# A two-layer encoder trunk: where a head's last norm, the splits, the rotation's sums and the latents' squares are computed

## The chip, the cores and the metric

One core of a Trainium2 chip. The metric is the device time of one execution of the program in microseconds; less is better. A core has engines that run beside each other: TensorE (PE, matmuls and transposes; its weight loads are listed as PEld), VectorE (DVE), ScalarE (ACT), GpSimd (POOL) and SyncE (SP), which here only issues DMA transfers. PE writes to PSUM, which the kernel divides into banks of 128 x 512 fp32 values; the other tiles lie in SBUF.

## The reference, cut to what matters

The model has 1024 tokens of width 1024, in fp32, and two layers. Each is a norm, a shift and scale from a conditioning vector, a token mixer with a SiLU gate, an output projection and a gated residual addition; a last norm closes it.

```python
for i in range(2):
    shift, scale, gate = _modulation(c, ada_w[i], ada_b[i])
    h = _rmsnorm(x, norm_g[i]) * (1.0 + scale) + shift
    y = _diff_attention(h, ...) if i == 0 else _mla(h, ...)
    x = x + gate * y
return _rmsnorm(x, final_norm_g)
```

Layer 0 is differential attention with 8 heads: q and k are rotated by position (`_rope`), each head has two softmaxes of which one is subtracted with a factor, and each head's output gets a norm of its own over its 128 channels:

```python
q, k, v, z = jnp.split(h @ w_in, 4, axis=-1)      # widths 1024 each
p = softmax(q1 k1) - lam * softmax(q2 k2)         # per head
o = _rmsnorm(p @ v, subln_g) * (1.0 - lambda_init)
y = (o.reshape(b, s, 1024) * jax.nn.silu(z)) @ w_out
```

Layer 1 is latent attention: q and k/v come from latents of 384 and 256 channels, and each latent is normed over its channels before it is multiplied on.

## The kernel before, in words

**Precision.** Every fp32 matmul is done as three fp32r matmuls of split operands: high times high, high times low and low times high (`mm3`, lines 182 to 184). So each operand needs a split: ScalarE copies it to a rounded high part, and GpSimd or VectorE subtracts this to get the low part. In `split_raw` (L227, L228) this is done for the projections' weights, in `Seven.put` (L1166, L1167) for the operands of the output projection.

**Order.** The program is written in Python; a planner then fixes each engine's order at build time, from its own simulated times and the order in which things were written. An engine's queue runs strictly in that order. Three helpers bind the planner: `tc.issue_after(ins)` puts what a block writes behind `ins` on the same engine; `behind(eng)` does so with the last copy or subtraction of the attention (`mk["S"]`, `mk["V"]`); `tc.keep_in_program_order(ins)`, in `in_turn`, pins an instruction behind everything written before it on its engine. `mk` is emptied after layer 0's attention, and with that `behind` and `in_turn` bind nothing.

**Layer 0's attention** (`attn0`, from L1002). Per head there are eight query tiles of 128 rows. A tile has two rounds of scores (L844), each with a maximum on VectorE (L397) and an exponential on ScalarE (L399), and VectorE joins the two (L852). One tile later the joined tile is transposed by PE in two groups of four (`transpose_p`, L380), copied by ScalarE (L382) and its low part made by VectorE (L383); two tiles later it is multiplied with v. Between these pieces, `fills` says how many steps of the next head's projections are put in; after each step `side.tick()` runs one entry of a list of side work. `rope` (L312) does the rotation there: ScalarE copies the projection (L319, L321), four DMAs swap its halves (L323), GpSimd multiplies it by the cosine (L324) and the swapped one by the sine (L329), and `fin` adds the two on VectorE (L333). `stack_k` and `stack_q` then split the sum (ScalarE L341, L342, L349, L350; GpSimd L343, L344, L351, L352).

**A head's own norm** (`subln`, L911). PE sums the squares by matmuls with a column of ones (L922), VectorE and GpSimd turn them into factors (L925 to L930, the power at L169), and `finish` (L876) brings the factors to all partitions: by two DMAs through DRAM (L405, L407), GpSimd multiplying after them (L882) and a store (L886), or, for the last half of the last head, which is wanted at once, by four diagonal matrices (VectorE, L899), matmuls with ones into a bank `rb` (L900), and a multiplication on VectorE (L901).

**Output projection of layer 0.** The product is done by Strassen's scheme with seven half-size products (`Seven`). Product n needs left factors A(n, h) and weights W(n, h), h = 0 to 3; for n = 2 to 5 the left factors are sums and differences of heads. `fetch_a` and `fetch_w` load them (L1150, on SP), `split_a` and `split_w` split them. During the last head, `extra0(i)` (L1259) is called after each tile i (8 to 10 are the tail after the eighth): it loads, splits (`both`), and starts `PRE0[i]` portions of products 0 and 1 by `Pre7.step`, one portion being three matmuls of 512 columns into one of two banks. These portions fill PE where the last head has no projections left.

After the attention, the rest of product 0 goes to the y banks 2 and 3, product 1 to two acc banks and two "tr" banks (`Z`, read to x by `add0`, L1376). Meanwhile `tail_b` runs `finish` for the last half head and the four sums and differences made of it (L1332 to L1335), which give A(2, 3) to A(5, 3). Product 2 follows in the y banks 0 to 3, then 3 to 6. In PSUM at this stage: four y banks, two tr banks, two acc banks. `group0` (L1382) norms x for layer 1 (`norm_x`: VectorE L454 or ScalarE L452, on tiles of 128 x 1024), and PE transposes it (L465).

**Layer 1's latents** (`lora`, L1601). Each projection half-strip of eight `mm3` is copied to `craw` and squared (L1611, L1614) by ScalarE; VectorE sums the squares over the latent's strips (L1615). At step `NORM_AT` of the following half, `norm` sums them over the partitions by PE (L1620), and the factors go through DRAM.

Of the kernel before, what the change touches and what calls it, by code (L numbers as in the profile page):

```python
# [16 lines left out]
ALU = mybir.AluOpType  # L17
# [4 lines left out]
P = 128  # L22
# [22 lines left out]
V_LATE = 6  # L45
MODS = (2, 1, 1, 1, 0, 0, 0, 0)
V1_AT = (3, 2)
NORM_AT = 4
PRE0 = (0, 0, 0, 0, 1, 1, 2, 2, 2, 3, 3)
PRE1 = (0, 0, 0, 0, 0, 0, 0, 1, 1, 1, 1)  # L50
LAST1 = (((0, 1), 0, HF), ((2,), 0, HF), ((3,), 0, 256), ((3,), 256, HF))
Z_LAST = 2
# [29 lines left out]
def trunk(ctx: ExitStack, tc: tile.TileContext, A, out):  # L82
# [226 lines left out]
                self.count += 1  # L309
                side.tick()  # L310

    def rope(rp, acc, half, scale, eng=G):  # L312

        cs = slice(half * HF, half * HF + HF)
        raw = rp.tile([P, HF], F32, name="rp_raw", tag="rp", bufs=6)
        sw = rp.tile([P, HF], F32, name="rp_sw", tag="rp", bufs=6)
        r = rp.tile([P, HF], F32, name="rp_r", tag="rp", bufs=6)
        if scale == 1.0:
            S.copy(raw, acc)  # L319
        else:  # L320
            S.mul(raw, acc, scale)  # L321
        for q in range(4):
            SP.dma_start(sw[q * 32 : q * 32 + 32], raw[(q ^ 1) * 32 : (q ^ 1) * 32 + 32])  # L323
        r_ = eng.tensor_mul(r, raw, cosT[:, cs])  # L324
        if eng is G:
            in_turn(r_)

        def rot():
            in_turn(G.tensor_mul(sw, sw, sinT[:, cs]))  # L329

        def fin():
            with behind("V"):
                V.tensor_add(r, r, sw)  # L333
            return r

        return rot, fin
# [38 lines left out]
    def transpose_p(p, pth, ptl, t, kh):  # L375

        tr = bank("tr", "tr", [P, 4, P])
        for j in range(4):
            kt = kh * 4 + j
            PE.transpose(tr[:, j, :], p[:, kt * P : (kt + 1) * P], ident)  # L380
        dst = slice(t * P, (t + 1) * P)
        mk["S"] = S.copy(pth[kh][:, :, dst], tr).ins  # L382
        mk["V"] = V.tensor_sub(ptl[kh][:, :, dst], tr, f32v(pth[kh][:, :, dst])).ins  # L383
# [364 lines left out]

    def k_done(h):
        def f(acc, half):  # L750
            rot, fin = rope(wp, acc, half, 1.0, G if h else V)

            def g():
                t = a0a.tile([P, 2, HF], F32R, name="ks", tag="ks", bufs=4)
                stack_k(t, fin())
                KS.setdefault(h, [None, None])[half] = t

            side.add(*[None] * ROT, rot, *[None] * (DEF - 1 - ROT), g)
        return f

    def q_done(h):
        def f(acc, half):
            rot, fin = rope(wp, acc, half, SC0, G if h else V)

            def g():
                qa = a0a.tile([P, 2, HF], F32R, name="qa", tag="qs", bufs=4)
                qb = a0a.tile([P, 2, HF], F32R, name="qb", tag="qs", bufs=4)
                stack_q(qa, qb, fin())
                QS.setdefault(h, [None, None])[half] = qa, qb

            side.add(*[None] * ROT, rot, *[None] * (DEF - 1 - ROT), g)
        return f
# [103 lines left out]
    def finish(o, y, l, h, half, dst, ap_, dgs):  # L876

        if dst is None:
            b, rb = bcast_rows(ap_, y, "osq", 4)

            def scale():
                in_turn(G.tensor_mul(t3(o), t3(o), rb))  # L882
                hooks.append(lambda: hooks.append(store))

            def store():
                SP.dma_start(oF[l][h, half], o)  # L886

            if l == 0 and (h, half) >= (NH - 2, 1):
                hooks.append(lambda: hooks.append(scale))
            else:  # L890
                hooks.append(scale)
            return
        rb = bank("z" if l else "tr", "rb", [P, HF])
        for j in range(4):
            js = slice(j * P, (j + 1) * P)
            if l:
                S.mul(dgs[:, js], ident, y[:, j : j + 1])
            else:
                V.tensor_scalar(dgs[:, js], ident, y[:, j : j + 1], None, op0=ALU.mult)  # L899
            PE.matmul(rb[:, js], ones, dgs[:, js], start=True, stop=True)  # L900
        V.tensor_mul(o, o, rb)  # L901

    ssq_at = []

    def head_out(o_, o, sq):

# [4 lines left out]
    def subln(o, sq, zz, half, h, dst):  # L911
# [5 lines left out]
            V.tensor_mul(o, o, GZ[h][half])  # L917

        def rest():
            pt = bank("tr", "ssq", [P, HF]) if dst is not None else ssq_at[0] if ssq_at else bank("acc", "ssq")  # L920
            for j in range(4):
                PE.matmul(pt[:, j : j + 1], sq[:, j * P : (j + 1) * P], ones[:, 0:1], start=True, stop=True)  # L922
            w = sm.tile([P, 4], F32, name="sl_w")
            fin = sm.tile([P, 4], F32, name="sl_f")
            V.tensor_mul(fin, zz, zz)  # L925
            V.scalar_tensor_tensor(out=w, in0=fin, scalar=P * EPS / GUARD ** 2, in1=pt[:, 0:4], op0=ALU.mult, op1=ALU.add)  # L926
# [3 lines left out]
            in_turn(G.tensor_mul(y, y, fin))  # L930
# [203 lines left out]
    class Seven:  # L1134
# [12 lines left out]
            self.raws[n, h, "W"] = self.load(self.home_w(n, h), tS[self.l][n, h])  # L1147

        def load(self, home, src):
            self.last = SP.dma_start(f32v(home[1]), src).ins  # L1150
            return *home, f32v(home[1])

        def split_a(self, n, h, eng=V):
# [47 lines left out]
    class Pre7:  # L1201
# [5 lines left out]
        def step(self):  # L1207
# [4 lines left out]
            if not h and not i:  # L1212
# [1 line left out]
                    self.done(self.accs)  # L1214
                self.accs = [bank("acc", "oy") for _ in range(2)]
                ssq_at.append(self.accs[1])
            self.sv.mm(n, self.accs[i], h, i, start=True)
            self.n += 1

    stX, stO = ExitStack(), ExitStack()  # L1220
# [38 lines left out]
    def extra0(i):  # L1259
# [34 lines left out]
        if i == 3:  # L1294
            fw(0, 2)
            fa(0, 2)
            fw(0, 3)
            SP.dma_start(k0["11"], oF[0][3, 0])
        if 3 <= i <= 6:
            both(0, i - 3)  # L1300
        if 4 <= i <= 6:
            fw(1, i - 4)
            fa(1, i - 4)
        if i == 6:
            SP.dma_start(k0["21"], oF[0][3, 1])
            k0["pair"] = [pw.tile([P, HF], F32, name="ob", tag="ob", bufs=4) for _ in range(4)]
        if i == 7:
            fw(1, 3)
            for t, (hh, half) in zip(k0["pair"], ((2, 0), (6, 0), (2, 1), (6, 1))):
                SP.dma_start(t, oF[0][hh, half])  # L1310
        if 7 <= i <= 9:
            both(1, i - 7)
        if i == 10:
            sv.split_w(1, 3)
            a11, a12, a21, a22 = k0["pair"]
# [66 lines left out]
    def group0(gi):  # L1382
        fulls = [[x_] for x_ in xf[4 * gi : 4 * gi + 4]]
        V.tensor_add(ssa[gi], ssa[gi], ssb[gi])
        norm_x(ssa[gi], fulls, (2, 3) if gi else ())

        def chunk(k):
            if gi == 1:
# [20 lines left out]
        sv0.fetch_a(2, h)  # L1409
    load_x0(0, 0)  # L1410
    Z = pre0.accs
    Y = [bank("y", "oy") for _ in range(4)]
    for h in range(4):
        for i in range(2, 4):
            sv0.mm(0, Y[i], h, i, start=True)
# [185 lines left out]
    def lora(idx, dst, gvec, width, ws=None, first=None):  # L1601
        n = len(idx)
        craw = [[None, None] for _ in range(n)]
        sums = [None, None]
        def put(i, half, acc):
            t = rpt("craw") if dst and i == 0 else lr.tile([P, HF], F32, name="craw", tag="craw", bufs=7)
            S.copy(t, acc)
# [4 lines left out]
            else:  # L1612
                s2 = rpt("csq")
                lm["S"] = S.activation(s2, acc, AF.Square).ins  # L1614
                lm["V"] = V.tensor_add(sums[half], sums[half], s2).ins  # L1615

        def norm(half):
            pt = bank("tr", "cps", [P, 4, P])
            for j in range(4):
                PE.matmul(pt[:, 0, j : j + 1], sums[half][:, j * P : (j + 1) * P], ones[:, 0:1], start=True, stop=True)  # L1620
# [716 lines left out]
```

## Time and profile before

| | us |
|---|---|
| median of three runs | 1432.95 |
| lowest and highest of them | 1429.36, 1434.21 |
| the profiled execution's own time | 1430.7 |
| its span, first to last instruction | 1428.9 |
| PE busy | 1380.7 |
| DVE, ACT, POOL busy | 970.2, 737.0, 720.0 |

The profile is of one execution. It gives each engine's busy time, groups of instructions by line (count, busy time, mean duration, idle time of the engine before them and what ended it), who waited for whom, a timeline, and a table by stage, whose rows are: from:to, length, then busy time and count of PE, PEld, DVE, ACT and POOL, the TensorE clock granted in the stretch (1 is full), the DMA engines' share and GB/s. A matmul in plain fp32, such as those with a column of ones, shows as two records. Matmuls overlap, so PE's busy time is no measure of how fast it works.

Stages, in us from the span's start: layer 0's norm and projections to about 171; its attention to 655, with the last head's tail to 702; the output projection to about 787; layer 1's projections to about 1000; its attention to about 1350; its output projection and the last norm to the end.

### The profile page before, as it was taken

Reading aid. Unit: us, or ns where it says so; the run is one execution under the profiler, and the core shown is the slowest. Engines: PE = TensorE matmul, PEld = TensorE weight load, DVE = VectorE, ACT = ScalarE, POOL = GpSimd, SP = SyncE. Lnnn points to the kernel's source line nnn. Section 1 sums busy time; section 2 is a strip of 40 time slices with the busy share of each in tenths; the row PEclk is TensorE's granted clock in tenths of the full one; section 3 lists DMA queues with packets and bytes.
Section 4 is the critical chain, followed back from the end, with each engine's and each line's share of the span. In section 5 each row is a group of like instructions: output and inputs, shape, how many; then the busy total and the mean of one; then the engine's idle time right before and its main releaser. Section 6 shows DMA issues by size and latency. Waiting matters only on the chain. (4 is left out here: it accounts for less than half of the span.)

```text
span 1428.9 us, 20757 instructions
## 1 busy us (share of the span) xinstructions
PE 1380.7 (97%) x7318; PEld 1149.6 (80%) x7318; DVE 970.2 (68%) x1383; ACT 737.0 (52%) x1325; POOL 720.0 (50%) x561
## 2 busy tenths in 40 slices
PE   8999999999999999999889999999999999999997
PEld 6777788888878788887767887787888888888886
DVE  8665778877777778677587876545666555555685
ACT  5523465656565556566536543335454454555554
POOL 5425264648585767564784233642131255653783
PEclk9999999999999999999999999999999999999999
DMA  9786634343443444424654136389444355566363
GB/s 345 245 243 196 191 103 131 89 143 104 147 141 113 136 127 121 148 79 166 206 185 155 45 90 215 121 283 257 145 132 119 103 165 190 180 212 210 132 252 118
DMA packets 149065, 231.52 MB, mean 162 GB/s; under 512 B 20577, under 2 KB 57569, under 8 KB 148962
## 3 DMA queue, kind: packets, MB, share of 16 engines
q1 hardware_dynamic: 148962, 230.21, 51.3%
q8 instruction: 57, 0.93, 0.3%
q14 instruction: 46, 0.38, 0.1%
HBM read 144.74 MB, written 61.81 MB: 145 GB/s over the span
## 5 line engine op out<-in xcount | busy, mean ns | idle before, releaser
L382 ACT CAST pth<-tr 128x512 fp32r<-128x512 f32 x256 | 150.4, 588 | 275.9 <-PE tr L380 272.2
L397 DVE TENSOR_REDUCE nm<-s 128x1 f32<-128x1024 f32 x192 | 233.7, 1218 | 67.2 <-PE s L844 55.3
L383 DVE TENSOR_TENSOR ptl<-tr,pth 128x512 fp32r<-128x512 f32 x256 | 176.0, 688 | 137.4 <-ACT pth L382 136.7
L228 POOL TENSOR_TENSOR wl<-wraw,wh 128x512 fp32r<-128x512 f32 (+2 forms) x79 | 104.7, 1327 | 203.8 <-ACT wh L227 190.7
L399 ACT ACTIVATE e<-s,nm 128x1024 f32<-128x1024 f32 x128 | 143.7, 1123 | 35.4 <-DVE nm L397 31.8
L380 PE MATMUL tr<-ident,e 128*128 128x128 f32 x1024 | 155.5, 274 | 5.4 <-DVE ptl L383 4.4
L380 PEld LDWEIGHTS tr<-ident,e 128*128 128x128 f32 x1024 | 120.2, 140 | 48.9 <-DVE ptl L383 25.1
L182 PE MATMUL acc<-h0h,wh 128*128 128x512 f32 x360 | 150.3, 418 | 1.8 <-DVE sl_w L926 0.9
L182 PE MATMUL pv<-pth,vt 128*128 128x256 f32 x512 | 147.4, 288 | 0.7 <-ACT pth L382 0.7
L183 PE MATMUL pv<-ptl,vt 128*128 128x256 f32 x512 | 145.8, 285 | 0.0
L184 PE MATMUL pv<-pth,vt 128*128 128x256 f32 x512 | 144.5, 282 | 0.0
L184 PE MATMUL acc<-h0h,wl 128*128 128x512 f32 x360 | 143.1, 397 | 0.6 <-POOL wl L228 0.6
L183 PE MATMUL acc<-h0l,wh 128*128 128x512 f32 x360 | 141.9, 394 | 0.0
L182 PEld LDWEIGHTS pv<-pth,vt 128*128 128x128 f32 x512 | 97.4, 190 | 3.7 <-ACT pth L382 0.9
L183 PEld LDWEIGHTS pv<-ptl,vt 128*128 128x128 f32 x512 | 97.6, 191 | 2.9
L184 PEld LDWEIGHTS pv<-pth,vt 128*128 128x128 f32 x512 | 97.6, 191 | 0.1
L324 POOL TENSOR_TENSOR rp_r<-rp_raw,cosT 128x512 f32<-128x512 f32 x38 | 50.2, 1322 | 93.0 <-ACT rp_raw L321 37.9
L329 POOL TENSOR_TENSOR rp_sw<-rp_sw,sinT 128x512 f32<-128x512 f32 x42 | 56.8, 1351 | 71.1 <-DMA rp_sw<-rp_raw 71.0
L1167 POOL TENSOR_TENSOR wol<-wol,woh 128x512 fp32r<-128x512 f32 x56 | 82.0, 1489 | 20.5 <-ACT woh L1166 20.5
L844 PE MATMUL s<-ks,qa 128*128 128x512 f32 x256 | 82.9, 405 | 4.3 <-DVE e L852 2.4
L852 DVE SCALAR_TENSOR_TENSOR e<-s,z,e 128x1024 f32<-128x1024 f32 x64 | 82.1, 1283 | 2.1
L184 PEld LDWEIGHTS acc<-h0h,wl 128*128 128x128 f32 x360 | 67.6, 188 | 16.3 <-POOL wl L228 1.1
(406 smaller groups left out, 3491.8 us busy)
## 6 DMA issues: line engine op xcount, KB each, us to landing
ada<-in_ada_ss SPq DMA_DIRECT2D x32, 512.0 KB, 5.4
wraw<-in_w_s SPq DMA_DIRECT2D x64, 256.0 KB, 2.8
vS<-v_hl SPq DMA_DIRECT2D x32, 512.0 KB, 6.0
vt<-vS SPq DMA_DIRECT2D x32, 512.0 KB, 4.1
wol<-tS SPq DMA_DIRECT2D x56, 256.0 KB, 4.8
tS<-ob SPq DMA_DIRECT2D x48, 256.0 KB, 2.0
rp_sw<-rp_raw SPq DMA_DIRECT2D x168, 64.0 KB, 2.0
bc_s<-bc_d SPq DMA_DIRECT2D x34, 256.0 KB, 3.9
```

Source lines behind the costliest of these rows:

```text
L182: PE.matmul(psum, ah, bh, start=first, stop=False, skip_group_check=skip)
L183: PE.matmul(psum, ah, bl, start=False, stop=False, skip_group_check=skip)
L184: mm3.last = PE.matmul(psum, al, bh, start=False, stop=last, skip_group_check=skip).ins
L228: sub = (V if pair_of else G).tensor_sub(l_[:, :n], raw[:, :n], f32v(h_[:, :n]))
L380: PE.transpose(tr[:, j, :], p[:, kt * P : (kt + 1) * P], ident)
L382: mk["S"] = S.copy(pth[kh][:, :, dst], tr).ins
L383: mk["V"] = V.tensor_sub(ptl[kh][:, :, dst], tr, f32v(pth[kh][:, :, dst])).ins
L397: mk["V"] = V.reduce_max(nm, s_ps, axis=AX.X, negate=True).ins
L399: mk["S"] = S.activation(e, s_ps, AF.Exp, bias=nm, scale=1.0, accum_out=zs).ins
L844: PE.matmul(s_ps[:, kc * HF : (kc + 1) * HF], src[:, c, ql], KS[h][kc][:, c, :], start=fst, stop=not fst)
L852: combined.append(V.scalar_tensor_tensor(out=e0, in0=e1, scalar=z1[:, 0:1], in1=e0, op0=ALU.mult, op1=ALU.add).ins)
L1167: sub = eng.tensor_sub(lo, raw, f32v(hi))
```

## The change

1. The last half head's norm: the sums of squares go to y bank 0 (`Y[0]`) and `rb` to y bank 1, both in place of "tr" banks; the diagonal matrices are made by ScalarE.
2. In `extra0` the splits of A and W are written earlier: h = 2 of product 0 with h = 1, h = 3 one tile sooner, those of product 1 one tile sooner; `PRE0` is changed, with the same sum of 14. Each portion is put behind the last transposes written. Loads of `Seven` for layer 0 and the loads in `extra0` are kept in program order on SP.
3. In layer 0 the rotation's final addition of heads 1 to 7 is done by GpSimd, in order (head 0 keeps VectorE throughout).
4. `group0(0)`: two of the four tiles of x are scaled by ScalarE.
5. In `lora` the last strip's squares are no longer added on VectorE: PE sums both tiles, with twice the matmuls. `NORM_AT` goes from 4 to 5.

```diff
-NORM_AT = 4
-PRE0 = (0, 0, 0, 0, 1, 1, 2, 2, 2, 3, 3)
+NORM_AT = 5
+PRE0 = (0, 0, 0, 0, 1, 2, 2, 2, 2, 2, 3)
...
-    def rope(rp, acc, half, scale, eng=G):
+    def rope(rp, acc, half, scale, eng=G, add=V):
...
         def fin():
-            with behind("V"):
-                V.tensor_add(r, r, sw)
+            if add is G:
+                in_turn(G.tensor_add(r, r, sw))
+            else:
+                with behind("V"):
+                    V.tensor_add(r, r, sw)
             return r
...
-            PE.transpose(tr[:, j, :], p[:, kt * P : (kt + 1) * P], ident)
+            transpose_p.last = PE.transpose(tr[:, j, :], p[:, kt * P : (kt + 1) * P], ident).ins
...
-            rot, fin = rope(wp, acc, half, 1.0, G if h else V)
+            rot, fin = rope(wp, acc, half, 1.0, *[G if h else V] * 2)
...
-            rot, fin = rope(wp, acc, half, SC0, G if h else V)
+            rot, fin = rope(wp, acc, half, SC0, *[G if h else V] * 2)
...
-        rb = bank("z" if l else "tr", "rb", [P, HF])
+        rb = bank("z", "rb") if l else Y[1]
         for j in range(4):
             js = slice(j * P, (j + 1) * P)
-            if l:
-                S.mul(dgs[:, js], ident, y[:, j : j + 1])
-            else:
-                V.tensor_scalar(dgs[:, js], ident, y[:, j : j + 1], None, op0=ALU.mult)
+            S.mul(dgs[:, js], ident, y[:, j : j + 1])
             PE.matmul(rb[:, js], ones, dgs[:, js], start=True, stop=True)
...
-            pt = bank("tr", "ssq", [P, HF]) if dst is not None else ssq_at[0] if ssq_at else bank("acc", "ssq")
+            pt = Y[0] if dst is not None else ssq_at[0] if ssq_at else bank("acc", "ssq")
...
         def load(self, home, src):
-            self.last = SP.dma_start(f32v(home[1]), src).ins
+            ins = SP.dma_start(f32v(home[1]), src)
+            self.last = ins.ins
+            if mk and not self.l:
+                tc.keep_in_program_order(ins)
             return *home, f32v(home[1])
...
-            self.sv.mm(n, self.accs[i], h, i, start=True)
+            with tc.issue_after(transpose_p.last):
+                self.sv.mm(n, self.accs[i], h, i, start=True)
             self.n += 1
...
-            SP.dma_start(k0["11"], oF[0][3, 0])
-        if 3 <= i <= 6:
-            both(0, i - 3)
+            tc.keep_in_program_order(SP.dma_start(k0["11"], oF[0][3, 0]))
+        for h in ((), (), (), (0,), (1, 2), (3,), (), (), (), (), ())[i]:
+            both(0, h)
...
-            SP.dma_start(k0["21"], oF[0][3, 1])
+            tc.keep_in_program_order(SP.dma_start(k0["21"], oF[0][3, 1]))
...
-                SP.dma_start(t, oF[0][hh, half])
-        if 7 <= i <= 9:
-            both(1, i - 7)
+                tc.keep_in_program_order(SP.dma_start(t, oF[0][hh, half]))
+        if 6 <= i <= 8:
+            both(1, i - 6)
...
-        norm_x(ssa[gi], fulls, (2, 3) if gi else ())
+        norm_x(ssa[gi], fulls, (2, 3) if gi else (1, 3))
...
-    Y = [bank("y", "oy") for _ in range(4)]
+    Y += [bank("y", "oy") for _ in range(4)]
...
-                lm["V"] = V.tensor_add(sums[half], sums[half], s2).ins
+                if i < n - 1:
+                    lm["V"] = V.tensor_add(sums[half], sums[half], s2).ins
+                else:
+                    last[half] = s2
...
             for j in range(4):
-                PE.matmul(pt[:, 0, j : j + 1], sums[half][:, j * P : (j + 1) * P], ones[:, 0:1], start=True, stop=True)
+                for t in (sums[half], last[half]):
+                    PE.matmul(pt[:, 0, j : j + 1], t[:, j * P : (j + 1) * P], ones[:, 0:1], start=t is sums[half], stop=t is last[half])
```

More of the change, by code (lines that the diff above doesn't have):

```diff
@@ L892, in finish @@
             return
-        rb = bank("z" if l else "tr", "rb", [P, HF])
+        rb = bank("z", "rb") if l else Y[1]
         for j in range(4):
             js = slice(j * P, (j + 1) * P)
-            if l:
-                S.mul(dgs[:, js], ident, y[:, j : j + 1])
-            else:
-                V.tensor_scalar(dgs[:, js], ident, y[:, j : j + 1], None, op0=ALU.mult)
+            S.mul(dgs[:, js], ident, y[:, j : j + 1])
             PE.matmul(rb[:, js], ones, dgs[:, js], start=True, stop=True)
         V.tensor_mul(o, o, rb)
-    ssq_at = []
+    ssq_at, Y = [], []
     def head_out(o_, o, sq):
@@ L1603, in lora @@
         craw = [[None, None] for _ in range(n)]
-        sums = [None, None]
+        sums, last = [None, None], [None, None]
         def put(i, half, acc):
```

## The prediction

> **What bounds the kernel now.** I read the page first, then who TensorE waited for, then the same by stage.
>
> ```profile
> span 1428.9 us, 20757 instructions
> PE 1380.7 (97%) x7318; PEld 1149.6 (80%) x7318; DVE 970.2 (68%) x1383; ACT 737.0 (52%) x1325; POOL 720.0 (50%) x561
> ```
>
> TensorE is busy for 1380.7 of 1428.9 us and no other engine for more than 970.2. So TensorE is the bound nearly everywhere, and its matmuls are not touched except for a few that are added. A gain can only come from the 48.2 us in which it stands still, and from stretches in which it runs slowly. The waits of PE name them:
>
> ```profile
> PE rb L900 <- DVE x L1376: 6.6, 1, 6.6
> PE tr L380 <- DVE ptl L383: 4.4, 6, 1.7
> PE oy L183 <- POOL wol L1167: 3.6, 3, 2.3
> PE s L844 <- DVE e L852: 2.4, 3, 1.3
> PE cps L1620 <- DVE csum L1615: 2.1, 1, 2.1
> PE trh L465 <- DVE x L454: 2.0, 2, 1.3
> ```
>
> The largest is one single wait. The table by stage shows where they lie, and one thing more, the clock (the number before the last two):
>
> ```profile
> 171.00:655.00 484.00, 477.18 (x2658) 401.42 (x2657) 364.12 (x506) 285.45 (x501) 302.16 (x244) 1.00 0.41 121
> 655.00:702.00 47.00, 39.74 (x223) 31.88 (x223) 29.22 (x44) 32.60 (x60) 28.75 (x24) 0.96 0.51 163
> 693.70:697.10 3.40, 3.40 (x10) 2.70 (x9) 0.69 (x1) 3.40 (x8) 3.40 (x4) 0.50 0.29 109
> 720.47:724.70 4.23, 4.23 (x15) 3.71 (x15) 2.41 (x3) 0.59 (x2) 2.16 (x2) 0.53 0.01 3
> 769.07:775.62 6.55, 6.55 (x28) 5.30 (x27) 3.54 (x6) 4.56 (x11) 3.08 (x3) 0.76 0.58 201
> 860.02:866.00 5.98, 5.98 (x23) 4.96 (x24) 5.75 (x9) 2.44 (x5) 5.43 (x2) 0.71 0.55 205
> ```
>
> 171 to 655 is layer 0's attention (6.8 us idle in 484), 655 to 702 its last head with the first portions of the output projection (7.3 idle in 47). The four short rows with a clock of 0.50 to 0.76 each begin just after a stall of PE. What the low clock costs is the length times what is missing of 1: 3.40 x 0.50 = 1.7 us, 4.23 x 0.47 = 2.0, 6.55 x 0.24 = 1.6, 5.98 x 0.29 = 1.7. So a stall removed there gives back its length and about 1.7 us more.
>
> The Trainium skill, "TensorE: Matmul & The Clock Gate", Part 1 (What's actually happening), says that the clock falls to half after an idle window of about 3.4 us. By that rule only the 6.6 us stall earns its slow stretch, and the sum below would be 5.0 us smaller. The trace has half clock after stalls of 2.1 us as well, so I go by the trace and keep the rule as a rival.
>
> **The change part by part**, against the profiled execution's own 1430.7 us (span 1428.9 and 1.8 around it).
>
> **A. Last head's norm in free banks.** The sums of squares and the broadcast factor rb move from the two "tr" banks to the y banks 0 and 1, which lie empty until the third product; the four diagonal tiles move from VectorE to ScalarE.
>
> ```profile
> 708.14 0.20 POOL L930 TENSOR_TENSOR rq_y<-rq_y,sl_f 128x4 f32<-128x4 f32 x1
> 708.38 5.03 DVE L899 TENSOR_SCALAR sq<-ident,rq_y 128x128 f32<-128x128 f32 x4 [1.18 <-POOL rq_y L930]
> 713.33 1.87 DVE L1376 TENSOR_TENSOR x<-x,oy 128x512 f32<-128x512 f32 x3
> 720.47 2.07 PE L900 MATMUL rb<-sq,ones 128*128 128x128 f32 x8 [6.62 <-DVE x L1376]
> 714.60 0.62 ACT L1166 CAST oah<-ob 128x512 fp32r<-128x512 f32 x1 [8.71 <-POOL ob L1119]
> 728.80 0.68 DVE L1334 TENSOR_TENSOR k<-sq,k 128x512 f32<-128x512 f32 x1
> ```
>
> ```profile
> 724.70:735.80 11.10, 11.10 (x50) 9.17 (x49) 10.90 (x11) 8.40 (x18) 7.55 (x5) 1.00 0.65 186
> ```
>
> (The row by itself is the third product's stretch in the table by stage.) The factors are known at 708.3 and the diagonals done at 713.4; rb then waits until 720.5 because its bank still holds a product that VectorE has not added to x. VectorE is late since the diagonals held it for 5 us. With bank Y[1] no such wait is left: PE waits for the diagonals only. On ScalarE, which had been idle for 8.71 us, the nearest row is the same operation in layer 1:
>
> ```profile
> L897 ACT ACTIVATE dg<-ident,zz x4: 392/397/403, 1337.1 to 1339.0; 128x128 f32<-128x128 f32 x4
> ```
>
> 4 x 0.4 = 1.6 us, done near 710, before PE ends the matmuls in front (720.47 - 6.62 = 713.85). Gain: 6.6 and the 2.0 of clock, **8.6**. What is late next: rb and the six matmuls left behind it take to about 716; the third product, at 11.1 us for its 48 matmuls, wants its fourth left factor three quarters later, near 724. That factor comes from L1334, which ended 9.0 us after rb began (729.5 against 720.5); with rb at 711 to 714 it is there at 720 to 723 and still has to be cast and split. This is close, so up to 2 us may come back here. The rest of VectorE's queue is relieved by 5 us just when PE comes 8.6 us earlier.
>
> **B. Splits a tile ahead, portions behind transposes, loads in program order.** Stretch 655 to 702 holds 7.3 us of idle and 1.7 of clock:
>
> ```profile
> PE oy L183 <- POOL wol L1167: 3.6, 3, 2.3
> PE tr L380 <- DVE ptl L383: 2.4, 3, 1.7
> PE pv L182 <- ACT pth L382: 0.7, 1, 0.7
> ```
>
> The first row is portions of the projection issued before GpSimd had split their weights. The others lie in the last tiles, where nothing is left to fill the wait for VectorE, since the portions have been used up earlier. A split one tile (about 6.5 us) ahead answers the first; holding portions behind the transposes leaves some for the end and answers the second. But the split of h = 3 keeps the same distance to its portion as the 2.3 us stall had, and the loads are now pinned behind whatever was written before them on SP:
>
> ```profile
> 651.88 0.92 SPq L1150 DMA_DIRECT2D oal<-oF  x2
> 654.56 0.32 SPq L405 DMA_DIRECT2D bc_d<-rq_y  x1
> 656.39 2.79 SPq L407 DMA_DIRECT2D bc_s<-bc_d  x1
> 668.63 0.43 SPq L1150 DMA_DIRECT2D wol<-tS  x1
> 678.12 0.32 SPq L405 DMA_DIRECT2D bc_d<-rq_y  x1
> ```
>
> The two loads at 651.88 stood ahead of a store that waits for the norm; they are written behind it and its broadcast, so they go out at 657 to 659, 5 to 7 us later, and the splits behind them too. The second store holds the queue from 669 to 678 in both kernels. Bounds: all 9.0 gone, or 6 lost. I take half, **4.4**, nearer to the rows that show idle PE, because the first portion is also moved back about one tile.
>
> **C. Latents' squares unsummed, norms one step later.** Four additions on VectorE go; each of four norms gets four more matmuls (eight records).
>
> ```profile
> 840.27 0.95 PE L1620 MATMUL cps<-ones,csum 128*128 128x1 f32 x8
> 841.08 0.48 PE L182 MATMUL acc<-h_h,wh 128*128 128x512 f32 x1
> ```
>
> Eight records hold PE for 0.81 us (841.08 less 840.27), so the cost is 4 x 0.81 = 3.2. Gone is the wait of 2.1 and its 1.7 of clock, since the last squares then come straight from ScalarE. **Gain 0.6**; between a loss of 3.2, if the wait stays, and 0.6.
>
> **D. Group 0's norm, two tiles of four on ScalarE.**
>
> ```profile
> 761.77 6.85 DVE L454 TENSOR_SCALAR x<-x,rq_y 128x1024 f32<-128x1024 f32 x4 [1.19 <-POOL rq_y L169]
> 791.02 2.19 ACT L452 ACTIVATE x<-x,rq_y 128x1024 f32<-128x1024 f32 x2 [1.59 <-POOL rq_y L169]
> ```
>
> Two tiles on each engine side by side: 3.4 against 2.2 us instead of 6.85. All four are ready near 765.2 instead of 768.6, and PE asked for the first at 766. The 2.0 of wait go with 1.6 of clock, **3.6**. ScalarE's casts of the last weights slip by 2.2 us; at worst, behind them, 2 us of the wait stay.
>
> **E. Rotation's sums on GpSimd**, heads 1 to 7 of layer 0: 28 additions.
>
> ```profile
> L333 DVE TENSOR_TENSOR rp_r<-rp_r,rp_sw 128x512 f32<-128x512 f32 x28 | 30.0, 1072 | 10.4 <-POOL rp_sw L329 10.2
> L329 POOL TENSOR_TENSOR rp_sw<-rp_sw,sinT 128x512 f32<-128x512 f32 x27 | 36.9, 1365 | 33.6 <-DMA rp_sw<-rp_raw 33.6
> L228 POOL TENSOR_TENSOR wl<-wraw,wh 128x512 fp32r<-128x512 f32 x39 | 50.5, 1296 | 37.0 <-ACT wh L227 35.8 <-POOL qb L352 0.9 <-PE tr L380 0.2
> PE tr L380 <- DVE ptl L383: 1.3, 2, 1.0
> PE acc L182 <- DVE sl_w L926: 0.9, 1, 0.9
> PE ssq L922 <- ACT rp_raw L321: 0.8, 1, 0.8
> ```
>
> (All in 171 to 655, where the 2.4 us for e lie too.) VectorE loses 30.0 us of work and 10.4 of standing in order behind GpSimd's product: what PE waits for there is VectorE's, 2.4 + 1.3 + 0.9, and 0.8 on ScalarE, whose copies follow it. That is 5.4; **I take 4.0**, between 5.4 and the loss of the rival below. GpSimd gets 28 x 1.37 = 38 us; its share in the stretch goes from 302 to 340 of 484 us, 70%. Queued behind each addition are the next weights' low parts (L228) and the next norm.
>
> The Trainium skill, "GPSIMD Engine Reference", section 4.1 (Engine selection), advises against this: a two-input addition belongs on VectorE and takes about twice as long on GpSimd. The trace has 1072 ns there and 1365 ns for the like product here; with a doubling to 2144 ns an estimate by that page would be 60 us of GpSimd work instead of 38.
>
> **Sum**: 8.6 + 4.4 + 0.6 + 3.6 + 4.0 = 21.2. Every pin and move changes the planner's order, and new waits come of it. I bound them between 0 and 10, four waits of the size of the largest but one (2.3), and take 4. Net 17.2: 1430.7 - 17.2 = 1413.5. The median of the three runs, 1432.95, lies 2.2 above the profiled execution, so I say **1415**; the forecast's own range is 1409 to 1421.
>
> **The rivals.**
>
> 1. *SP's order decides B.* The loads that go out 5 to 7 us later hold the portions, and PE stands in the last head instead: B turns from 4.4 gained to 6 lost, 1425. For it: the queue already stands for 9 us behind one store. Against: the portion waits one tile more by the diff. 15%.
> 2. *The clock falls anyhow.* The slow stretches of B, C and D stay or come back after shorter waits: 1.7 + 1.6 + 1.7 = 5.0 us less, 1420. It is what the skill's rule named above would give. For it: not every stall of 2 us in the trace has such a stretch behind it. Against: the three have. 8%.
> 3. *All goes and nothing comes*: 8.6 + 9.0 + 0.6 + 3.6 + 5.4 = 27.2, 1404 to 1406. 7%.
> 4. *A does not do what it says*: PE's queue has rb where it waits for something else, as the third factor's chain or the planner's place for it: 8.6 less, 1424. 4%.
> 5. *Slower: GpSimd's queue becomes the bound of layer 0.* Each addition, 1.37 us, delays the weights' low parts behind it, and PE takes it over. A, B, C, D and the 4 of new waits leave 13.2 of gain; from 10 of the 28 additions reaching PE whole the gain is gone, and with two thirds of them (26 us) it is 1446. For it: 70% busy, in stretches more. Against: PE waited for none of the 39 weights of this stretch. 6%.
>
> **How the numbers follow.** Forecast 60%, rivals 15, 8, 7, 4 and 6. About 0.3% (4.3 us) is what a measurement of this kernel can tell from no change. Below 1428.6 lie all cases but the last, less some tail of the first and fourth: faster 0.90, same 0.04, slower 0.06. The range 1406 to 1427 takes in the forecast, rivals 1, 2 and 4 and leaves out the fifth, most of the third and the tails, about 17%.
>
> **What would show it.** A: no wait of rb for x, clock 1.00 where 0.53 was, L899's place taken by ScalarE. B: no wait for wol, transposes of the last tiles without idle; the loads behind the store on SP. C: 64 records of cps instead of 32 and no wait for csum. D: no wait of trh for x. E: no VectorE row for the rotation in heads 1 to 7, and GpSimd at 70% there. The prediction is wrong if PE's idle in 655 to 702 is above 7, if waits for wl appear in layer 0, or if rb still waits.

## The result, and the profile after

Five runs of the changed kernel have a median of 1467.45 us (1463.51 to 1468.97), against 1432.95 before: a ratio of 1.0243 (95% interval 1.0222 to 1.0263). The change made the kernel slower by 35 us; the forecast was 1415.

The page of the changed kernel, its span and the first lines of its first part:

```profile
span 1467.1 us, 20749 instructions
PE 1393.6 (95%) x7350; PEld 1159.1 (79%) x7350; DVE 937.8 (64%) x1345; ACT 739.3 (50%) x1331; POOL 752.9 (51%) x589
```

PE is busy for 12.9 us more than before and stands still for 73.5 us (1467.1 less 1393.6) instead of 48.2. VectorE lost 32.4 us of work, with 38 operations fewer, and GpSimd got 32.9 us, with 28 more. The waits of PE over the whole execution of the changed kernel:

```profile
PE tr L383 <- DVE ptl L386: 18.2, 14, 4.7
PE s L847 <- DVE e L855: 14.7, 9, 3.3
PE ssq L922 <- ACT rp_raw L321: 6.2, 2, 4.8
PE oy L183 <- POOL wol L1170: 5.4, 3, 2.5
PE trh L468 <- DVE h L477: 4.7, 4, 2.2
...
PE oy L182 <- DVE o L901: 1.6, 1, 1.6
```

The waits for rb, csum and x are gone. In their place stand waits of layer 0's attention: for VectorE's low parts of P and its joined tiles (4.4 and 2.4 us before) and for ScalarE. The table by stage from the first score matmul of head 0 to that of head 7, before and then after (columns as in the section on the time before):

```profile
143.10:629.60 486.50, 479.48 (x2641) 402.26 (x2640) 363.60 (x505) 282.60 (x496) 293.09 (x236) 1.00 0.42 126
```

```profile
143.50:667.10 523.60, 488.98 (x2639) 410.21 (x2638) 336.39 (x478) 282.11 (x496) 322.78 (x263) 0.98 0.40 117
```

This stage alone is 37.1 us longer; the whole span grew by 38.2. PE's idle time in it rose from 7.0 to 34.6 us, and its busy time by 9.5 with the same number of matmuls, since the granted clock fell from 1.00 to 0.98. All the rest of the kernel together is 1.1 us longer. So the loss lies in seven heads of layer 0, where only part E, the rotation's sums, does anything.

Who waits for those sums? ScalarE's waits in this stage, before (171 to 655) and after (175 to 660):

```profile
ACT qa L349 <- DVE rp_r L333: 15.9, 10, 2.8
ACT ks L341 <- DVE rp_r L333: 9.7, 8, 3.8
```

```profile
ACT qa L352 <- POOL rp_r L333: 34.0, 10, 5.6
ACT ks L344 <- POOL rp_r L333: 27.0, 11, 6.5
```

ScalarE stacks each rotated half (`stack_k`, `stack_q`) and stood 25.6 us for the sum when VectorE made it; now it stands 61.0 us. The longest of these waits, in the changed kernel's timelines of GpSimd, ScalarE, VectorE and PE (start, duration; the idle time before a row and what ended it in brackets):

```profile
486.70 1.29 POOL L329 TENSOR_TENSOR rp_sw<-rp_sw,sinT 128x512 f32<-128x512 f32 x1 [3.16 <-DMA rp_sw<-rp_raw]
487.94 1.29 POOL L1088 TENSOR_TENSOR ob<-ob 128x512 f32<-128x512 f32 x1
489.31 1.29 POOL L1090 TENSOR_TENSOR ot<-ob,ob 128x512 f32<-128x512 f32 x1
490.56 1.29 POOL L333 TENSOR_TENSOR rp_r<-rp_r,rp_sw 128x512 f32<-128x512 f32 x1
...
491.88 0.62 ACT L344 CAST ks<-rp_r 64x512 fp32r<-64x512 f32 x1 [6.48 <-POOL rp_r L333]
...
493.17 1.09 ACT L402 ACTIVATE s<-s,nm 128x1024 f32<-128x1024 f32 x1
...
494.50 0.16 DVE L853 RECIPROCAL z<-z 128x1 f32<-128x1 f32 x1 [8.61 <-ACT s L402]
...
496.95 0.66 PE L383 MATMUL tr<-ident,e 128*128 128x128 f32 x4 [4.65 <-DVE ptl L386]
```

The sine product ended near 488.0, and the sum could have begun there. But GpSimd's queue holds two operations on the output projection's weights (`ob`, `ot`) that were written between product and sum, so the sum begins at 490.56. ScalarE's copy, next in its queue, starts at 491.88 after a wait of 6.48 us; the exponential behind it starts at 493.17, VectorE has stood for 8.61 us for that exponential, and PE for 4.65 us for VectorE. Nothing in this chain is long; it is four queues that each run in order.

### The profile page after: what moved, and what is told of

It is laid out like the page before. It is cut to its first block, busy times and chain, and to the rows that moved or that the text cites. A ratio compares the mean times of both kernels' runs of the same rounds, so it can differ in the third digit from the quotient of the medians.

```text
span 1467.1 us, 20749 instructions
## 1 busy us (share of the span) xinstructions
PE 1393.6 (95%) x7350; PEld 1159.1 (79%) x7350; DVE 937.8 (64%) x1345; ACT 739.3 (50%) x1331; POOL 752.9 (51%) x589
## 5 line engine op out<-in xcount | busy, mean ns | idle before, releaser
L847 PE MATMUL s<-ks,qb 128*128 128x512 f32 x256 | 83.9, 406 | 0.0
```

Source lines behind the costliest of these rows:

```text
L847: PE.matmul(s_ps[:, kc * HF : (kc + 1) * HF], src[:, c, ql], KS[h][kc][:, c, :], start=fst, stop=not fst)
```

## The experiments

A ratio is against the kernel before on the same chip, with its 95% interval. Line numbers are each kernel's own.

### The loss is part E's

**All parts but E** (`e1_rope_back`): the changed kernel with `rope` as before.

> The changed kernel with the rotation's sums back on VectorE, all other parts kept. Theory 1 (the sums on GpSimd make ScalarE's copies wait in layer 0's attention) and rival 2 (GpSimd has too much work there): the start of the last head comes back from 667 to about 630 us, the whole to about 1430. Rival 3 (loads in program order and portions behind transposes are to blame): it stays above 1455.

Measured: 1431.03 against 1430.98, ratio 1.0010 (0.9997 to 1.0023).

**E alone** (`e2_rope_only`): the kernel before with `rope` as changed.

> The kernel before with the rotation's sums on GpSimd and nothing else. Theory 1 and rival 2: about 1468 us, ScalarE's copies L341 and L349 wait about 60 us for the sums instead of 26 for VectorE's. Rival 3: about 1433.

Measured: 1467.26, ratio 1.0260 (1.0242 to 1.0278). E alone costs all of it, and A, B, C and D together bring nothing.

### Order or load

**The sum written directly behind the sine product** (`e3_rope_early`), with all parts:

```diff
             in_turn(G.tensor_mul(sw, sw, sinT[:, cs]))
+            if add is G:
+                in_turn(G.tensor_add(r, r, sw))
```

> The changed kernel with the same sums on GpSimd, written directly behind the sine product, three side ticks ahead of the copies; GpSimd's work is the same. Theory 1 (what counts is the other GpSimd work written between product and sum, which the sum has to stand behind while ScalarE waits): the wait of the copies falls below 25 us and the time to 1430 to 1440. Rival 2 (GpSimd's 36 us of added work): it stays above 1455.

Measured: 1440.79, ratio 1.0075 (1.0059 to 1.0092). ScalarE's waits (171 to 655) and the same stage as above:

```profile
ACT qa L352 <- POOL rp_r L331: 22.0, 11, 4.8
...
ACT ks L344 <- POOL rp_r L331: 8.2, 5, 3.4
```

```profile
144.00:638.90 494.90, 480.30 (x2638) 402.88 (x2637) 338.37 (x478) 281.64 (x496) 324.03 (x263) 1.00 0.41 123
```

The same additions on the same engine, only further ahead in its queue, give back 24 of the 35 us (10.7 are left, by the ratio): ScalarE waits 30.2 us instead of 61.0, PE is idle for 14.6 instead of 34.6. Both wait and time lie just outside what the theory said (below 25 us, at most 1440), so something was left to explain.

**The waiting copies put later instead** (`e9_stack_late`): the sum stays where the change has it.

```diff
             def g():
-                t = a0a.tile([P, 2, HF], F32R, name="ks", tag="ks", bufs=4)
-                stack_k(t, fin())
-                KS.setdefault(h, [None, None])[half] = t
+                r = fin()
+
+                def stack():
+                    t = a0a.tile([P, 2, HF], F32R, name="ks", tag="ks", bufs=4)
+                    stack_k(t, r)
+                    KS.setdefault(h, [None, None])[half] = t
+
+                side.late.append([3, stack]) if h else stack()
```

(`tick` runs `stack` three steps later; q likewise.)

> The changed kernel with all its parts; only ScalarE's two stacking copies of each rotated half (ks, qa, with GpSimd's low parts and the transfers behind them) are written three strip steps later than the sum, for heads 1 to 7. The sum stays on GpSimd at the place it has in the changed kernel, and GpSimd's work stays the same. Theory (the loss of 36 us comes about because ScalarE's copies stand in ScalarE's queue for GpSimd's late sum, 61 us of waits there, and the exponentials and copies of P behind them starve VectorE and TensorE): by three steps, some 4 us, later the sum is nearly always there; ScalarE's waits for rp_r fall below 25 us, as they are before, and the time comes to 1433 to 1445. Rival (GpSimd's own load of 34 us more, or its queue, holds TensorE by another way, such as the weights' low parts or the low parts of k and q): the waits of ScalarE go but the time stays above 1460. Second rival: the copies now come too late for the scores of the next head and TensorE waits for ks or qa: above 1467.

Measured: 1435.09 against 1432.07, ratio 1.0023 (1.0008 to 1.0038). ScalarE's waits (171 to 660) and the stage:

```profile
ACT qa L357 <- POOL rp_r L338: 14.0, 6, 4.2
ACT ks L349 <- POOL rp_r L338: 10.6, 7, 3.2
```

```profile
145.70:640.40 494.70, 482.26 (x2647) 407.48 (x2645) 336.42 (x478) 282.29 (x497) 322.92 (x264) 0.99 0.42 124
```

GpSimd's load and the place of the sum in its queue stay as they were; what goes later is the copies, the low parts that GpSimd makes behind them, and their transfers. The loss falls from 35 us to 3.3 (by the ratio; this profiled execution lies 5.6 us above the median). So the loss reaches PE through the copies that wait for the sum, and the timeline above shows the path behind them, ScalarE's exponentials. What share GpSimd's low parts, later too, have in it, no run separates.

**The load alone** (`e12_load_only`): the kernel before, with an addition on GpSimd that nobody reads at each place of a sum.

```diff
+            if extra:
+                in_turn(G.tensor_add(raw, raw, raw))
             with behind("V"):
                 V.tensor_add(r, r, sw)
```

> The kernel before, rotation's sums on VectorE as they were; GpSimd gets 28 additions more of 128x512 (the raw tile with itself, a result that nobody reads) at the places in its queue where the changed kernel has the sums, heads 1 to 7. So GpSimd carries the load of part E, some 36 us, and no other engine waits for it. Theory (E costs by the order in which ScalarE waits for the sum, not by the load): within 6 us of before, 1430 to 1437. Rival (GpSimd's load, by what is queued behind it there or by what VectorE loses when both work at once, makes the 36 us): 1450 or more.

Measured: 1443.17 against 1431.37, ratio 1.0073 (1.0057 to 1.0090). This is between both expectations, and above what I allowed: the load is not free. It was even a little smaller than part E's: its 28 additions, with one tile as both inputs, take 31.8 us in all, those of part E some 36 (28 x 1.29). ScalarE's wait for VectorE's sums rose from 25.6 to 34.8 us. VectorE's sums in this kernel and in the next (171 to 650; 30.0 us, 1072 ns and 10.4 us of waits before):

```profile
L335 DVE TENSOR_TENSOR rp_r<-rp_r,rp_sw 128x512 f32<-128x512 f32 x28 | 34.4, 1230 | 14.8 <-POOL rp_sw L329 14.7
```

```profile
L340 DVE TENSOR_TENSOR rp_r<-rp_r,rp_sw 128x512 f32<-128x512 f32 x28 | 34.8, 1244 | 17.2 <-POOL rp_sw L334 17.2
```

**The load with late copies** (`e15_load_late`: `e12_load_only` with the copies of `e9_stack_late`), and **late copies alone** (`e14_late_alone`), the control.

> The kernel before with 28 additions more on GpSimd that nobody reads, and the stacking copies three steps later. The additions alone cost 10.4 us (ratio 1.0073). Theory (that load too reaches TensorE by ScalarE's copies, which wait for a sum that is later because the sine products stand longer in GpSimd's queue and VectorE's sums get longer, 1230 ns against 1072): with later copies at most 4 us are left, 1430 to 1436. Rival (the load costs by VectorE's slower additions or by GpSimd's other results, whatever ScalarE's order): 1438 to 1443, as with the additions alone.

Measured: 1440.50 against 1430.08, ratio 1.0070 (1.0058 to 1.0082).

> The kernel before, sums on VectorE, with one change: the stacking copies of heads 1 to 7 three strip steps later. It is the control for the runs in which later copies took away most of the loss: is the later place a gain by itself, without any work moved? Theory (TensorE's 7.0 us of idle between the scores of head 0 and of head 7 are all that could be won there, and ScalarE's 25.6 us of waits for the sum were covered): within 4 us of before, 1427 to 1433. Rival (the later place is worth as much as it brought back elsewhere, since it always shortens ScalarE's queue): below 1425.

Measured: 1434.70, ratio 1.0033 (1.0020 to 1.0045). The late place is no gain, it costs 4.6 us, more than either expectation had it: PE then waits for transfers and for VectorE (171 to 650):

```profile
PE s L859 <- DVE e L867: 4.0, 4, 1.5
PE s L859 <- DMA qa<-qa: 3.6, 3, 2.3
```

So the 32 us of `e9_stack_late` come from waits removed, not from the place; by the ratios, what part E with late copies still loses (1.0023) is no more than the late place costs by itself (1.0033). For the load my theory fell, 1440.50 against at most 1436: ScalarE waits for almost no sum in `e15_load_late` (3.6 us), yet the kernel is as slow as with the load alone. Against its control the load costs 5.8 us there (1440.50 less 1434.70) and not 10.4, so a part of it may have gone through the copies. The rest is not placed: VectorE has sums of 1244 ns and 17.2 us of standing for GpSimd's products, and the added operations hold the raw tile's buffer longer, so that ScalarE once waited for one of them:

```profile
ACT zth L795 <- POOL rp_raw L338: 4.3, 1, 4.3
```

**Early sum and late copies**, with all parts (`e10_early_late`) and with E alone (`e16_rope_early_late`).

> The changed kernel with all its parts; the sum on GpSimd directly behind its sine product, and the stacking copies two strip steps later than the sum's old place. Putting the sum early left 9.8 us of the 36 us loss, putting the stacking later left about 3. Theory (what the early sum left is still ScalarE's wait for it, 30 us against 25 before): ScalarE's waits for rp_r fall below 10 us and the time comes to 1428 to 1436. Rival (what is left is GpSimd's load, since the sine products and weights' low parts come later): 1438 to 1442, as with the early sum alone.

Measured: 1435.34 against 1431.37, ratio 1.0027 (1.0016 to 1.0038). The theory holds: ScalarE waits 6.1 us for the sums.

> Part E alone, with the sum directly behind its sine product and the stacking copies two steps later; no other part of the change. With all parts this order gave 3.9 us more than before. Theory (what is left comes from the last head, where part B keeps its own waits, and from transfers of q that come late): 1429 to 1434. Rival (VectorE's 30 us of relief are worth something once ScalarE waits for nothing): below 1428.

Measured: 1431.94 against 1430.08, ratio 1.0015 (1.0007 to 1.0024). With ScalarE hardly kept waiting (4.7 us for the sums), part E costs 2 us; the 30 us that it takes off VectorE win nothing even then. PE waits there for transfers of q (3.0 us) and, once, for a weight's low part (2.5 us).

### Where the gains of A to D went

**A alone** (`e4_banks_only`).

> The kernel before with the last head's norm in y banks 0 and 1 and its diagonals on ScalarE, nothing else. By the prediction's term: rb no longer waits, 8.6 us less, about 1424. Rival: waits of 1.4 to 1.7 us for weights, for the multiplied head and for its fourth factor, as the changed kernel shows them in the third product, give half back, about 1428.

Measured: 1430.66, ratio 0.9998 (0.9989 to 1.0007). Its waits between 715 and 740, and the clock behind them:

```profile
PE oy L182 <- DVE o L898: 3.8, 1, 3.8
PE oy L183 <- POOL wol L1164: 1.3, 1, 1.3
```

```profile
723.99:730.00 6.01, 6.01 (x15) 4.80 (x16) 6.01 (x6) 4.17 (x8) 3.78 (x3) 0.55 0.19 58
```

The 6.6 us for rb are gone; 5.1 come back within ten us. PE's third product starts in y bank 1, and rb lies there until VectorE has multiplied with it; that stands in VectorE's queue behind five additions to x and four left factors. The slow stretch stays too.

**A with that product first in VectorE's queue** (`e11_banks_o_first`): `issue_after` it for the other additions and VectorE's left factors.

> The kernel before with part A (norm of the last head in free banks), and with one thing more: VectorE's product o times rb is put ahead of the additions of oz to x and of the third product's left factors, so that the bank Y[1], in which rb lies, is read at once. With part A alone TensorE waited 3.8 us for that product before it could start the third product in that bank, and 1.3 us for wol, with the half clock behind. Theory (the gain of A is held back by that place in VectorE's queue): the wait for o falls from 3.8 to below 1 us; gain 3 to 6 us, 1425 to 1428. Rival (GpSimd's splits of the third product's weights set the place anyway): the wait for o goes, waits for wol or oal grow by as much, and the time stays within 1.5 us of 1431.

Measured: 1431.72 against 1432.07, ratio 0.9989 (0.9979 to 0.9999): a gain of 1.6 us, 3.0 at most, the only version whose interval lies below 1. What came is the rival's account: the wait for o is gone, those for the left factor's low part (oal) have grown. PE's waits between 715 and 740 are these, with VectorE's and GpSimd's timelines of that time:

```profile
PE oz L184 <- DVE oal L1166: 2.7, 2, 2.0
PE oy L184 <- DVE oal L1166: 2.7, 3, 2.0
```

```profile
715.00 0.69 DVE L898 TENSOR_TENSOR o<-o,oy 128x512 f32<-128x512 f32 x1 [4.28 <-PE oy L897]
715.61 1.50 DVE L1166 TENSOR_TENSOR oal<-oal,oah 128x512 fp32r<-128x512 f32 x1
717.04 1.77 DVE L1331 TENSOR_TENSOR sq<-k,o 128x512 f32<-128x512 f32 x1
...
725.51 0.67 DVE L1375 TENSOR_TENSOR x<-x,oy 128x512 f32<-128x512 f32 x1
```

```profile
715.27 13.15 POOL L1166 TENSOR_TENSOR wol<-wol,woh 128x512 fp32r<-128x512 f32 x8
```

The next bound is VectorE's and GpSimd's work itself: while GpSimd makes the low parts of eight weights (13.15 us, 1.64 us each where one takes 1.29 elsewhere), an operation of VectorE on two tiles takes 1.77 us instead of 0.68. The Trainium skill, "SBUF — State Buffer", section "SBUF: two separate sides", says that VectorE operations with two SBUF inputs and GpSimd share a pair of ports that one of them holds for a whole instruction; these rows agree with it. VectorE's last row, in the midst of the same subtractions, takes only 0.67 us; one of its inputs (oy) lies in PSUM.

**B alone** (`e7_portions_only`), **D alone** (`e5_norm_only`), **C alone** (`e6_squares_only`).

> The kernel before with part B alone: splits a tile ahead, portions behind the transposes, loads in program order. The prediction's term is a gain of 4.4 us. Theory (the last head's waits are only exchanged: the wait for e grows because the casts of the weights stand before the exponential on ScalarE): within 1.5 us of before, 1429.5 to 1432.5. Rival (B is what loses the gain of the others, as the prediction's first rival said of SP's order): slower by 3 to 6 us, 1434 to 1437.

Measured: 1432.60 against 1432.07, ratio 0.9999 (0.9987 to 1.0012). PE's waits between 655 and 740, and what ScalarE did before the exponential that PE waited for:

```profile
PE s L844 <- DVE e L852: 4.9, 2, 4.4
PE oy L183 <- POOL wol L1170: 4.0, 2, 2.5
PE rb L900 <- DVE x L1380: 3.9, 1, 3.9
```

```profile
661.76 0.62 ACT L1169 CAST woh<-wol 128x512 fp32r<-128x512 f32 x1 [2.81 <-DMA wol<-tS]
662.28 1.08 ACT L399 ACTIVATE s<-s,nm 128x1024 f32<-128x1024 f32 x1
```

The cast stands ahead of an exponential here (behind it before) and waits 2.81 us for its weight: the exponential, VectorE's joining and PE wait with it. This is the first weight of all, whose split part B writes at the same tile as before. What is late is its load, which is now kept in program order on SP. SP's first loads of weights, in the kernel before and in this one:

```profile
630.14 1.24 SPq L1150 DMA_DIRECT2D wol<-tS  x2
```

```profile
655.63 0.42 SPq L1150 DMA_DIRECT2D wol<-tS  x1
...
658.72 1.81 SPq L1150 DMA_DIRECT2D wol<-tS  x1
```

Two loads that went out at 630 before now stand behind the store and, the second, behind its broadcast, 25 to 28 us later. So SP's order, the prediction's first rival, does delay the last head; the time stays the same, and among the waits that fall is that for rb, from 6.6 to 3.9 us. An engine's queue with a late head holds up what stands behind it, as in part E.

> The kernel before with part D alone: group 0's norm with two of four tiles on ScalarE. The prediction's term is a gain of 3.6 us. Theory after the first runs (the four small parts together gave nothing, since each removed wait is taken over by another one close by): the wait of the transposes for x goes, but waits for h, whose cast on ScalarE comes later, take its place: gain 0 to 1.5 us, 1429.5 to 1431. Rival (D gives its 3.6 and another part loses it): 1427 to 1428.

Measured: 1433.28 against 1432.07, ratio 1.0004 (0.9993 to 1.0014). The waits for x are gone; PE stands at 776.32, where ScalarE's cast of a weight waits for its load (ScalarE's row of the kernel before, then this kernel's rows):

```profile
773.78 1.25 ACT L227 CAST wh<-wraw 128x512 fp32r<-128x512 f32 x2 [1.71 <-DMA wraw<-in_w_s]
```

```profile
774.03 0.62 ACT L227 CAST wh<-wraw 128x512 fp32r<-128x512 f32 x1 [2.28 <-DMA wraw<-in_w_s]
...
776.32 0.63 PE L465 MATMUL trh<-ident,x 128*128 128x128 f32 x4 [2.11 <-DVE h L474]
```

That load comes at 774 in both kernels. What was won before it is waited away there: 2.0 us went, 2.11 came.

> The kernel before with part C alone: the latents' last squares unsummed, norms one step later. The prediction's term is a gain of 0.6 us, between a loss of 3.2 and that. Theory (one wait of 2.1 us goes, 32 more matmul records of 0.1 us come): 1430 to 1432.5. Rival (the norm one step later makes the rows behind it late): 1434 to 1436.

Measured: 1432.82 against 1431.37, ratio 1.0004 (0.9996 to 1.0013). The two sums of the norm's matmuls:

```profile
L1625 PE MATMUL cps<-ones,csum x32: 164/250/250, 835.3 to 870.7; 128*128 128x1 f32 x32
...
L1625 PE MATMUL cps<-ones,csq x32: 164/250/250, 835.5 to 870.9; 128*128 128x1 f32 x32
```

The wait for csum is gone and 32 records have come. From the first matmul of layer 1 to the first of z it is 99.7 us (788.4 to 888.1) instead of 100.1 (787.5 to 887.6): 0.4 us, which the times cannot tell from nothing.

**A, C and D with o first** (`e13_three_o_first`).

> The kernel before with parts A, C and D, and VectorE's product o times rb ahead of the additions and the third product's left factors: all of the change that can gain, without B and E. A with o first alone gave a ratio of 0.9989. Theory (between the last head and layer 1 VectorE's own queue, at 1.77 us for an operation on two tiles while GpSimd works, sets the pace; a wait that is removed is given back a few us later): the gains don't add, 1428.5 to 1431. Rival (each part gives its term once the others are in): 1420 to 1426.

Measured: 1433.25 against 1431.37, ratio 1.0014 (1.0004 to 1.0023), 2.0 us slower and above both expectations. The gains do not add. PE's waits for rb, o, csum and x are gone; between 655 and 900 it waits for VectorE's left factors (5.6 us) and for h (3.5 us) instead. Why it is slower and not the same is not shown.

## Why the prediction was wrong

**E** failed, and decides everything: forecast a gain of 4.0, measured alone a loss of 37 (1.0260). The step that failed is the question of who is behind whom. I named what is queued behind each new addition on GpSimd (weights' low parts, the next norm), and not what the addition itself would stand behind. ScalarE's copies, which read the sum, I counted only as a wait of 0.8 us to be gained. `fin` is written four steps after `rot`, and everything that GpSimd was given in between stands ahead of the sum, since the sum is pinned in order (an addition on GpSimd without that pin was not run). ScalarE already stood 25.6 us for this sum when VectorE made it; behind GpSimd it stood 61.0. I had bounded the edit by PE's waits (5.4 us), as if nothing else hung on it, and none of the signs that I named for a wrong prediction lies on this path. Most of it is the order: two different cures, with the same additions left on GpSimd, give back 24 and 32 of the 35 us. The load alone costs 10 beside VectorE's own sums; with the sums moved, and early sum and late copies, 2 are left. Even without E the forecast would have failed: A to D were to bring 13.2 us after the allowance, and `e1_rope_back` shows none.

**Rival 5** had the right engine and sign (1446, chance 6%), but the wrong reader: the waits of PE in this stage of the changed kernel name no weight's low part at all, but VectorE and ScalarE. It priced an addition at its length, 1.37 us (measured 1.29). The price was its place in the queue, up to 6.48 us of ScalarE's time at once, and a slower clock behind stalls (0.58 from 496.95 to 501.00, right after the 4.65 us above). GpSimd's share in the stage rose from 60 to 62%, not to 70, since the stage grew with it. The Trainium skill, "GPSIMD Engine Reference", section 4.1, advised against the move. The result goes its way, but by the place in the queue and not by the duration of which the page speaks: with the order cured, the same additions cost 2 us. Its doubling holds against an undisturbed VectorE (1.29 us against 0.68), not against the 1.07 us that the sum took here.

**A**: the mechanism was right (no wait for rb), the term of 8.6 was mis-sized: measured 0.3 (between 1.6 gained and 1.0 lost), and 1.6 with o first. I wrote that up to 2 us may come back by the fourth left factor; it was the bank itself, which rb now occupies where the product starts, and behind it VectorE at 1.77 us an operation.

**B**: 4.4 forecast, nothing measured. The loads behind the store went out as foreseen (657 to 659 in `e1_rope_back`), and rival 1's delay came, though not its loss of 6 us. I had read two late loads from SP's rows (651.88) and overlooked the two loads of weights at 630, which go out 25 to 28 us later; and I had not counted that ScalarE's casts, which wait for them, can stand ahead of the exponentials. Nor is 4.4 the middle of my bounds (9.0 gained, 6 lost), which is 1.5: I had halved the gain alone.

**C**: 0.6 forecast, 0.4 in the trace. The mechanism is as foreseen, a wait gone for 32 records more; the term is too small for the times to confirm (ratio 1.0004, 0.9996 to 1.0013).

**D**: 3.6 forecast, nothing measured. The worst case that I named, 2 us left behind ScalarE's casts, came in size but not in its way: the casts were to slip by 2.2 us, and this one starts 0.25 us later only (774.03 against 773.78), held by its load.

The allowance of 4 us for new waits was far too small: A, B and D each gave back all they took. Rival 2 was right that slow stretches stay, for another reason: in `e4_banks_only`, `e5_norm_only` and `e7_portions_only` they begin behind a new wait.

## To carry over

When an operation moves to another engine, look at three places before its duration: what stands between its input and its new place in that queue, who reads its result, and what stands behind that reader in its own queue. What a wait in one engine costs is what it holds up in the engine that bounds the kernel (here 4.65 us of PE for 6.48 us of ScalarE, and a slower clock behind). And where PE is busy for 97%, a removed stall is a gain only as far as nothing else close behind it (a bank, a load, a cast) is late too.

## What the runs showed of the hardware

VectorE's additions of two tiles in SBUF and GpSimd's operations lengthen each other: VectorE's took 0.68 us with GpSimd idle (728.80 before) and 1.77 beside a solid row of GpSimd's subtractions, which then took 1.64 instead of 1.29. The rotation's sums before are a mixture, 0.68 to 2.04 us with a mean of 1.07; with 28 more additions on GpSimd the mean is 1.23 to 1.24. The diagonals of part A, only 128x128, took 1.29 to 1.33 us each on VectorE while GpSimd worked without a break. So work put on an "idle" GpSimd costs VectorE too. And the half clock can come after stalls of some 2 us: with D alone, right behind the 2.11 us wait,

```profile
777.00:780.40 3.40, 3.18 (x11) 2.15 (x9) 1.74 (x3) 3.10 (x7) 2.06 (x2) 0.51 0.62 189
```

0.51 for 3.4 us, though not after every stall of that length.
